# Projecting queries and keys from tokens read in residue order, with joined masks, PSUM-fed pooled sums and a GpSimd scale, in an eight-core decoder layer

## The chip, the cores and the metric

The kernel runs on all 8 cores of one Trainium2 chip. Each core computes 2,048 of the 16,384 tokens of the layer, and reads the 2,048 tokens before them as a halo. The metric is the device time of the slowest core, in microseconds (us).

Some executions fall into a slower state, in which the cores of one die, or of both, have a lower granted TensorE clock. Experiments ran on four chips, called A to D below, and each of them timed the kernel before beside the changed ones. A ratio is the mean time of one kernel's fast runs over the mean of the other's fast runs of the same rounds, so it is not quite the ratio of the medians that are quoted. Intervals are 95% intervals.

## The reference, cut to what matters

```python
ATTN_GROUPS = ((128, 1), (512, 4), (2048, 16))   # (window, dilation) of groups 0, 1, 2; 4 heads of 64 each

def reference(x, ...):                            # x (1, 16384, 1024)
    h = rms_norm(x, g_pre_mix)
    proj = h @ w_in                               # q, k, v (768 columns each), u (256), gates (2 x 1024)
    q, k = apply_rope(q), apply_rope(k)           # t1*cos - t2*sin, t2*cos + t1*sin
    # per group: positions p are split into `dilation` residue streams p mod dilation;
    # within a stream a causal band of 128 steps: softmax(q k / 8) v
    # the three groups are joined by the sums of their softmax denominators
    y_pool = multiscale_pool(u, ...)              # trailing mean over 2/4/8/16 tokens, minus the token
    merged = gate_a * (o_attn @ w_proj_attn) + gate_p * (y_pool @ w_proj_pool)
    x = x + rms_norm(merged @ w_out, g_post_mix)
    h2 = rms_norm(x, g_pre_ffn)
    a, b = split(h2 @ w_gate_up)                  # 2 x 2816
    return x + rms_norm((silu(a) * b) @ w_down, g_post_ffn)
```

Groups 1 and 2 need their queries and keys ordered by residue: all tokens with p mod 4 = 0 first, then 1, 2, 3, and the same modulo 16. The question is which engine should do that shuffle.

## The kernel before

The normed tokens are kept feature-major as `hT` and `hTh` (halo), bf16, 128 partitions x 8 chunks x 2,048 tokens. A first stage norms and transposes the tokens and projects group 2 (12 units of two 8-matmul products, each unit 512 tokens). It ends with the halo part of groups 0 and 1. Four attention stages of 512 tokens follow, `s` = 0 to 3, then the merge, the output projection and the feed-forward part. In the profile PE runs matmuls, DVE is VectorE, ACT ScalarE and POOL GpSimd.

A projection with its rotary step: two products into a pair of PSUM banks, four VectorE products with the cosine and sine tables, and two GpSimd sums. The sums do the shuffle: they read fp32 tiles in steps of 64 bytes (`v_r`) or 16 bytes (`v_rho`) and write contiguous or blocked bf16.

```python
    def rope(ring, wa, wb, rhs, tn, dst_a, dst_b, view, n=512, t0=0):
        tb = tab(tn)
        b = ring.new()
        cos, sin = tb[:, 0, t0:t0 + n], tb[:, 1, t0:t0 + n]
        mm8(b[:, 0, 0:n], wa, rhs)          # 8 matmuls; rhs(k) is the moving operand
        mm8(b[:, 1, 0:n], wb, rhs)
        for dst, fa, fb, op in ((dst_a, cos, sin, ALU.subtract), (dst_b, sin, cos, ALU.add)):
            t = rt.new()
            dve.tensor_tensor(out=t[:, 0, 0:n], in0=b[:, 0, 0:n], in1=fa, op=ALU.mult)
            dve.tensor_tensor(out=t[:, 1, 0:n], in0=b[:, 1, 0:n], in1=fb, op=ALU.mult)
            pool.tensor_tensor(out=dst, in0=view(t[:, 0, 0:n]), in1=view(t[:, 1, 0:n]), op=op)

    v_r = lambda t: t.rearrange("p (a r) -> p r a", r=16)
    v_rho = lambda t: t.rearrange("p (j rho) -> p rho j", rho=4)

    def qk2_unit(kind, s, halo):            # group 2
        # ... (weights and destinations)
        rope(any2, ..., lambda k: src[:, k, s * 512:(s + 1) * 512], s + 4 * halo, da, db, v_r)

    def f1(s, r1, r2):                      # groups 0 and 1, s = -1 (halo) to 3
        # ...
        rhs = lambda k: src[:, k, c0:c0 + 512]
        # ... rope(r2, ..., rhs, tn, ..., v_rho) for q of both groups and k of group 1
```

One attention step, the end of an attention stage, and the pooled branch:

```python
        act.activation(out=pt[:, :, :], in_=sb[:, :, :], func=AF.Exp, scale=0.125)     # att_qk
        for hh in range(2):
            dve.tensor_tensor(out=pt[:, hh, :], in0=pt[:, hh, :], in1=masks[:, mask, :], op=ALU.mult)
        # ...
            dve.tensor_tensor(out=oT2[s % 3][:, pair, :].rearrange(...), in0=val..., in1=den..., op=ALU.mult)
        # ... pooled(s)
                dve.scalar_tensor_tensor(out=zT[p, :], in0=Sx[p, 16:UL], scalar=invw[p, c:c + 1],
                                         in1=X[p, 16:UL], op0=ALU.mult, op1=ALU.subtract)
```

The kernel records all operations first. A list scheduler then orders each engine's instructions from a cost per operation (`op_cost`) and the buffers' lifetimes. All instructions are therefore issued from one or two lines of a helper, and the groups of the profile are told apart by their tiles.

The softmax here doesn't subtract the row's maximum and nothing guards it: scores larger than these inputs give would overflow.

## Time and profile before

The kernel before took 1035.36 us (median of 3, 1034.27 to 1035.75). The profiled execution took 1024.27 us.

| stretch | end | what it holds |
|---|---|---|
| first stage | 146.9 us | norms, transposes, group 2, halo |
| attention, merge, output projection | 547.6 us | stages 0 to 3 and what follows |
| feed-forward | 1022.7 us | matmuls back to back |

The first and second parts of the page: busy time of each engine, then its busy tenths in 40 equal slices of 25.6 us.

```profile
span 1022.7 us, 15344 instructions; the slowest of 8 cores (1018.5 to 1022.7 us)
PE 930.7 (91%) x5520; PEld 472.5 (46%) x5520; DVE 420.4 (41%) x573; ACT 346.4 (34%) x556; POOL 352.7 (34%) x350
...
PE   2779898989787988999989999999999999999993
...
DVE  5668448679998343433455211211112121121111
...
PEclk9899999999999989999999999999999999999997
```

PE is busy at 90% or more in almost every slice of the second half. In slices 11 to 13 it falls to seven or eight tenths, and there, in slices 10 to 12, DVE shows three nines in a row.

Windows of the trace give the same by stretch. The columns are: window and length; busy us (and instructions) of PE, PEld (weight loads), DVE, ACT, POOL; mean granted clock; DMA share; GB/s.

```profile
0.00:150.00 150.00, 114.16 (x849) 76.67 (x850) 88.46 (x144) 85.34 (x161) 66.99 (x55) 0.95 0.71 188
...
225.00:325.00 100.00, 85.89 (x713) 49.21 (x711) 92.55 (x126) 40.46 (x61) 58.39 (x42) 0.97 0.17 30
```

In 225:325, inside attention, VectorE is busy 92.6 of 100 us, and PE 85.9. The groups of instructions show what that consists of (busy us, mean ns of one, then idle time before and what ended it). A matmul's length here is modelled and longer than its spacing: 379 ns stands for a matmul that starts 216 ns after the one before.

```profile
L596 PE MATMUL ps<-hT_68,wq_66_108 128*128 128x512 bf16 x112 | 27.9, 390 | 0.9 <-DVE rt_73_115 L594 0.9
...
L596 PE MATMUL ps<-hT_68,wk_50_92 128*128 128x512 bf16 x56 | 13.4, 379 | 0.0
...
L594 POOL TENSOR_TENSOR q_0_64_106<-rt_73_115 128x512 bf16<-128x512 f32 x5 | 10.8, 2168 | 13.8 <-DVE rt_73_115 L594 12.4 <-DVE uX_88_130 L594 1.4
```

The first line is queries of groups 0 and 1, the second keys of group 2, the third a rope sum of 2.17 us. The view of one tile gives the spread of the mask products (ns, shortest, median, longest):

```profile
L594 DVE TENSOR_TENSOR PT_75_117<-PT_75_117,masks_44 x48: 406/420/3747, 154.4 to 376.6; 128x512 bf16<-128x512 bf16 x48
```

A mask takes 420 ns if nothing disturbs it, yet up to 3,747. The timeline (start us, length us) shows one such meeting:

```profile
242.66 2.15 POOL L594 TENSOR_TENSOR q_0_64_106<-rt_72_114 128x512 bf16<-128x512 f32 x1 [7.24 <-DVE rt_72_114 L594]
243.03 2.40 DVE L594 TENSOR_TENSOR PT_75_117<-PT_75_117,masks_44 128x512 bf16<-128x512 bf16 x2
```

Two masks, 0.84 us by the median, took 2.40 us: the GpSimd sum ran until 244.81, and the masks ended 0.62 us later. The Trainium skill, "SBUF — State Buffer", section Who interferes with whom, describes this as a port pair that VectorE's second SBUF input shares with GpSimd under an exclusive lock, and this trace agrees: on every one of the eight cores 24 of the 96 masks took more than half as long again as the median, and each of them ended 0.28 to 0.29 us after a GpSimd instruction ended.

Weight loads for the values of group 2 read the tokens in steps of 32 bytes, and the tile view has them at 143 ns, where a contiguous load of the same 128x128 takes 98:

```profile
L596 PEld LDWEIGHTS ps<-wv_51_93,hTh_69 x112: 142/143/151, 124.1 to 138.0; 128*128 128x128 bf16 x112
```

The chain of waits that ended last, by engine, as shares of the span:

```profile
PE 72%; DVE 9%; issue 7%; POOL 6%; ACT 5%; DMA 1%; DVEq 0%; POOLq 0%; ACTq 0%; SPq 0%
```

### The profile page before, as it was taken

What the parts mean: (1) busy time and instruction counts of PE and PEld (TensorE: products, weight loads), DVE (VectorE), ACT (ScalarE), POOL (GpSimd) and SP (SyncE); (2) the same over time, 40 slices, a digit from 0 to 9 for tenths busy, and PEclk for the clock granted to TensorE, in tenths of its full rate; (3) what the DMA queues carried; (4) which work ended last, traced back from release to release, by engine and by line L of the source; (5) the groups of instructions that cost most, each with busy time, mean ns of one, the idle gap of its engine ahead of it and who ended that gap; (6) DMA issues with size and microseconds to landing.
All of it is one profiled execution on the core that took longest, in us unless ns stands there. A gap on an engine that the chain in (4) does not pass through costs nothing.

```text
span 1022.7 us, 15344 instructions; the slowest of 8 cores (1018.5 to 1022.7 us)
## 1 busy us (share of the span) xinstructions
PE 930.7 (91%) x5520; PEld 472.5 (46%) x5520; DVE 420.4 (41%) x573; ACT 346.4 (34%) x556; POOL 352.7 (34%) x350
## 2 busy tenths in 40 slices
PE   2779898989787988999989999999999999999993
PEld 2346585556453443444444444444444444444441
DVE  5668448679998343433455211211112121121111
ACT  4686437645343242422766111111101111111110
POOL 1528445344757512333886110111332000001232
PEclk9899999999999989999999999999999999999997
DMA  8868711220061635331777667663323444430321
GB/s 234 261 188 217 172 30 43 31 54 1 1 114 22 99 59 121 62 62 22 208 263 225 117 116 124 119 109 62 124 104 122 83 79 69 80 62 1 124 83 41
DMA packets 30778, 105.02 MB, mean 103 GB/s; under 512 B 3952, under 2 KB 3952, under 8 KB 30704
## 3 DMA queue, kind: packets, MB, share of 16 engines
q0 software_dynamic: 14432, 45.65, 26.9%
q1 hardware_dynamic: 15984, 58.33, 17.1%
q8 instruction: 45, 0.74, 0.3%
q14 instruction: 29, 0.24, 0.1%
q10 hardware_dynamic: 288, 0.06, 0.1%
HBM read 132.90 MB, written 16.78 MB: 146 GB/s over the span
## 4 chain that ended last, share of the span: by engine, by line
PE 72%; DVE 9%; issue 7%; POOL 6%; ACT 5%; DMA 1%; DVEq 0%; POOLq 0%; ACTq 0%; SPq 0%
PE ps L596 63%; PE ps L594 9%; DVE PT_75_117 L594 2%; ACT xsb_53_95 L594 1%; DVE PT_74_116 L594 1%; DVE rt_72_114 L594 1%; DVE zT_134 L594 1%; DVE rt_73_115 L594 1%; DMA xst_37_79<-xo 1%; POOL x1b_101_143 L594 1%; POOL x1b_102_144 L594 1%; DVE hTh_69 L594 1%; POOL x1b_103_145 L594 1%; ACT junk_55_97 L594 1%; ACT PT_75_117 L594 0%
## 5 line engine op out<-in xcount | busy, mean ns | idle before, releaser
L596 PE MATMUL ps<-wdna_155,ffT_154 128*128 128x512 bf16 x512 | 115.7, 379 | 0.0
L596 PE MATMUL ps<-hT_68,wgu_109_151 128*128 128x512 bf16 x420 | 100.4, 379 | 0.0
L596 PE MATMUL ps<-hT_68,wgu_110_152 128*128 128x512 bf16 x420 | 100.4, 379 | 0.0
L596 PE MATMUL ps<-hT_68,wgu_111_153 128*128 128x512 bf16 x392 | 93.7, 379 | 0.0
L596 PEld LDWEIGHTS ps<-wdna_155,ffT_154 128*128 128x128 bf16 x512 | 50.1, 98 | 60.4
L596 PEld LDWEIGHTS ps<-hT_68,wgu_109_151 128*128 128x128 bf16 x420 | 41.0, 98 | 49.3
L596 PEld LDWEIGHTS ps<-hT_68,wgu_110_152 128*128 128x128 bf16 x420 | 41.0, 98 | 49.1
L596 PEld LDWEIGHTS ps<-hT_68,wgu_111_153 128*128 128x128 bf16 x392 | 38.4, 98 | 46.2
L596 PE MATMUL ps<-hT_68,wgs_76_118 128*128 128x512 bf16 x224 | 56.3, 393 | 2.9 <-ACT tg_80_122 L594 1.8
L596 PE MATMUL ps<-hT_68,wgs_77_119 128*128 128x512 bf16 x224 | 53.5, 379 | 2.1 <-ACT tg_81_123 L594 1.0
L594 DVE TENSOR_TENSOR ffT_154<-ps,sa_115_157 128x512 bf16<-128x512 f32 x30 | 20.7, 691 | 79.2 <-PE ps L594 79.2
L594 DVE TENSOR_TENSOR ffT_154<-ps,sa_116_158 128x512 bf16<-128x512 f32 x29 | 20.1, 692 | 78.4 <-PE ps L594 78.4
L594 DVE TENSOR_TENSOR ffT_154<-ps,sa_117_159 128x512 bf16<-128x512 f32 x29 | 20.1, 691 | 77.1 <-PE ps L594 77.1
L594 ACT ACTIVATE sa_115_157<-ps 128x512 f32<-128x512 f32 x30 | 17.9, 598 | 80.1 <-PE ps L594 80.1
L594 ACT ACTIVATE sa_116_158<-ps 128x512 f32<-128x512 f32 x29 | 17.3, 597 | 80.8 <-PE ps L594 80.8
L594 ACT ACTIVATE sa_117_159<-ps 128x512 f32<-128x512 f32 x29 | 17.3, 597 | 78.0 <-PE ps L594 78.0
L594 DVE TENSOR_TENSOR PT_75_117<-PT_75_117,masks_44 128x512 bf16<-128x512 bf16 x48 | 39.6, 864 | 8.6 <-ACT PT_75_117 L594 8.5
L594 ACT ACTIVATE junkd_107_149<-ps 128x1024 bf16<-128x1024 f32 x18 | 18.3, 1016 | 73.2 <-PE ps L594 73.1
L594 DVE SCALAR_TENSOR_TENSOR tg_80_122<-tg_80_122,ps 128x512 f32<-128x512 f32 x32 | 22.0, 689 | 46.8 <-ACT tg_80_122 L594 44.1
L596 PE MATMUL ps<-wdnb_156,ffT_154 128*128 128x512 bf16 x160 | 39.8, 379 | 0.0
L594 DVE SCALAR_TENSOR_TENSOR tg_81_123<-tg_81_123,ps 128x512 f32<-128x512 f32 x32 | 22.0, 687 | 40.4 <-ACT tg_81_123 L594 40.3
L594 ACT ACTIVATE junkd_108_150<-ps 128x1024 bf16<-128x1024 f32 x14 | 14.2, 1017 | 69.4 <-PE ps L594 69.4
(499 smaller groups left out, 1821.6 us busy)
## 6 DMA issues: line engine op xcount, KB each, us to landing
wgu_109_151<-wgu POOLq DMA_DIRECT2D x15, 512.0 KB, 5.8
wgu_110_152<-wgu POOLq DMA_DIRECT2D x15, 512.0 KB, 5.8
wgu_111_153<-wgu POOLq DMA_DIRECT2D x14, 512.0 KB, 5.7
wgs_76_118<-wg POOLq DMA_DIRECT2D x8, 512.0 KB, 5.3
wgs_77_119<-wg POOLq DMA_DIRECT2D x8, 512.0 KB, 6.1
wdna_155<-wdn POOLq DMA_DIRECT2D x8, 512.0 KB, 8.6
tab_70_112<-tab SPq DMA_DIRECT2D x6, 512.0 KB, 6.0
tab_71_113<-tab SPq DMA_DIRECT2D x6, 512.0 KB, 6.1
```

Source lines behind the costliest of these rows:

```text
L594: e.ops.append(lambda q, m=method, a=a, k=k, s=sem.sem, v=step: getattr(q, m)(*a, **k).then_inc(s, v))
L596: e.ops.append(lambda q, m=method, a=a, k=k: getattr(q, m)(*a, **k))
```

## The change

The intent was to take the shuffle off GpSimd, whose sums lock VectorE out, and give it to PE's reads. Each matmul then reads its 512 tokens in residue order, so that PSUM, tables and sums are all contiguous. VectorE is relieved three more ways. The scheduler learns of the shared port.

```diff
 # residue order: PE reads in steps of 16 elements (32 bytes) or 4 elements (8 bytes)
+    by16 = lambda t: t.rearrange("p (a r) -> p r a", r=16)
+    by4 = lambda t: t.rearrange("p (j rho) -> p rho j", rho=4)
-        rope(any2, ..., lambda k: src[:, k, s * 512:(s + 1) * 512], s + 4 * halo, da, db, v_r)
+        rope(any2, ..., lambda k: by16(src[:, k, s * 512:(s + 1) * 512]), tb[:, 0, :], tb[:, 1, :], da, db)
-        rhs = lambda k: src[:, k, c0:c0 + 512]
+        rhs = lambda k: by4(src[:, k, c0:c0 + 512])
+        if s < 0:
+            rhs = lambda k: by16(src[:, k, c0:c0 + 512])
-            pool.tensor_tensor(out=dst, in0=view(t[:, 0, 0:n]), in1=view(t[:, 1, 0:n]), op=op)
+            pool.tensor_tensor(out=dst, in0=fap(t[:, 0, 0:n], w), in1=fap(t[:, 1, 0:n], w), op=op)
 # ... (tables permuted on the host to match; k0 is written through by4 instead)

 # masks in one op, the mask broadcast over the two heads with a zero step
-        for hh in range(2):
-            dve.tensor_tensor(out=pt[:, hh, :], in0=pt[:, hh, :], in1=masks[:, mask, :], op=ALU.mult)
+        dve.tensor_tensor(out=pt[:, :, :], in0=pt[:, :, :], in1=fap(masks[:, mask, :], [(0, 2), (1, 512)]), op=ALU.mult)

 # final scale on GpSimd; pooled sums with the token's term read from PSUM (u), not SBUF (X)
-            dve.tensor_tensor(out=oT2[s % 3][:, pair, :]..., op=ALU.mult)
+            pool.tensor_tensor(out=oT2[s % 3][:, pair, :]..., op=ALU.mult)
-                dve.scalar_tensor_tensor(out=zT[p, :], ..., in1=X[p, 16:UL], ...)
+                dve.scalar_tensor_tensor(out=zT[p, :], ..., in1=u[p, :], ...)

 # scheduler: a VectorE op with two SBUF inputs and a GpSimd op exclude each other
+        if n.port:
+            t = max(t, self.pool.free)
+        elif n.eng is self.pool and not n.dma:
+            t = max(t, self.port_free)
-    return 0.17 + (0.0034 if strided else 0.0021) * n
+    return 0.17 + (0.0040 if strided else 0.0021) * n

 # weight loads of the next stage paced one token tile later
-        if i >= NT and todo and i + 3 < 2 * NT:
+        if i >= NT and todo and i + 4 < 2 * NT:
-            pool.dma(d, w, dsem("d_w01_%d" % len(todo)), after=[sp_x[i + 3]])
+            pool.dma(d, w, dsem("d_w01_%d" % len(todo)), after=[sp_x[i + 4]])
 # ... (smaller moves: two copies to GpSimd, the order of four adds, own semaphores for the last weight loads)
```

## The prediction

> **What bounds the kernel now.** From about 550 us to the end, matmuls run back to back at 216 ns per 128x512 (timeline); nothing in the change reaches that part. Before it PE loses time: from the matmuls' columns at 216 ns per 512 I estimate 118 us of PE idle in the first 500 us, 50 in 0:150 (norms, group-2 queries and keys; DMA share 0.71) and about 50 in 150:325 (attention). There VectorE is tightest: 148.5 of 175 us busy, 92.5 of 100 in 225:325 (busy time by window). Much of that is waiting: a mask multiply takes 0.42 us at the median but up to 3.7; the 96 take 74 us, not 40 (groups by tile). The long ones end when a GpSimd rope sum ends. The Trainium skill ("SBUF — State Buffer", Who interferes with whom) says a VectorE instruction with two SBUF inputs contends with a GpSimd instruction that reads SBUF; the trace agrees: one pair took 2.40 us beside a 2.15 us sum, while products reading PSUM stay at 0.68.
>
> **What changes.**
> - Masks: 96 ops become 48. One alone should take about 0.69 us (0.42 plus 512 bf16 elements at two per cycle, the skill's "VectorE: DVE Perf Modes"; estimate), against 0.84 for two. With fewer waits I expect 74 us to become about 42.
> - Pooled sums: 16 subtractions (16 us, 0.74 to 2.7 each) read PSUM: about 12 us, no waits. A PSUM bank is held longer.
> - Final scale: 8 ops, 16 us (1.3 to 4.9 each), leave VectorE; GpSimd gets about 8 x 1.5 us.
> - Rope sums on GpSimd read contiguous tiles: 1.95 to 2.15 us become about 1.3 (the unstrided k0 form now): some 48 ops, 35 us less, shorter blocks for VectorE.
> - The scheduler now models the shared port and places masks between sums.
> VectorE in 150:325 falls from 148 to about 100 us; PE's work there, about 125 us, becomes the bound.
> - PE: moving operands are read with 32-byte steps (192 matmuls of group 2, and the halo) or 8-byte steps (256 of groups 0 and 1). No moving operand in the trace is read so. Weight loads are: 98 ns contiguous, about 113 with 8-byte steps, 144 with 32-byte steps. If 32-byte steps double a matmul, 46 us of PE work is added, mostly where PE has 50 us of slack; if 8-byte steps do too, another 55 us come in attention and the change loses. I take no penalty as likeliest.
>
> **On the critical path.** Of some 50 us of VectorE and 25 of net GpSimd relief I expect 28 us of the attention stage and 5 of the first to reach the end: about 1003 us. The possible stride penalty skews the range upwards.
>
> **What would show it.** Right: 128x512 matmuls on residue-order tokens still start 216 ns apart; joined masks near 0.7 us, few over 1.5; rope sums near 1.3 us; VectorE busy in attention below 110 us; merge starting some 30 us earlier; the last 450 us unchanged. Wrong: those matmuls 400 ns or more apart; masks still waiting; PE in attention waiting on ACT's exponentials or PSUM banks.
>
> **What would make it wrong.** A stride penalty on moving reads; the broadcast mask losing the two-per-cycle rate (1.2 us each); the scale's long GpSimd op delaying the merge; the new order losing elsewhere; or the attention chain (scores, exponential, mask, values, one score buffer) being latency-bound, so that a freer VectorE buys little.
>
> Chances: faster by over 2% 0.62, within 2% 0.2, slower by over 2% 0.18. Predicted 1003 us, range 975 to 1050.

## The result, and the profile after

The changed kernel is correct and took 1206.06 us (median of its four runs, 1204.56 to 1206.45 in the fast three; one slow run took 1344.45). The kernel before of the same rounds took 1035.29. The ratio is 1.1643 [1.1620, 1.1666]: slower by 16.4%.

```profile
span 1204.9 us, 15240 instructions; the slowest of 8 cores (1199.1 to 1204.9 us)
PE 1138.1 (94%) x5520; PEld 492.8 (41%) x5520; DVE 371.9 (31%) x509; ACT 346.3 (29%) x556; POOL 326.8 (27%) x366
...
PE   3899999899999989899999989999999999999994
...
DVE  5231233041334565553433454122111112221110
...
PEclk9999965677999999899999999999999999999997
```

PE has as many matmuls as before, 5,520, but is busy 207 us longer; DVE, ACT and POOL are busy as long or less. DVE no longer reaches nine tenths in any slice. The sixth to tenth slices show something new: a granted clock of five to seven tenths (the nines before them record nothing, as shown below). The first stage now ends at 303.2 us instead of 146.9, and the output projection at 729.8 instead of 547.6. The feed-forward part takes 475 us in both kernels (729.8 to 1204.9, and 547.6 to 1022.7). The chain of waits is now almost all PE:

```profile
PE 88%; issue 3%; POOL 3%; DVE 2%; ACT 1%; DMA 1%; SPq 0%; POOLq 0%; DVEq 0%; ACTq 0%
```

The same groups as before, and the masks by tile:

```profile
L610 PE MATMUL ps<-hT_68,wq_66_108 128*128 128x512 bf16 x112 | 53.2, 628 | 1.0 <-DVE rt_72_114 L608 1.0
...
L610 PE MATMUL ps<-hT_68,wk_50_92 128*128 128x512 bf16 x56 | 52.8, 1097 | 0.0
...
L608 POOL TENSOR_TENSOR q_0_64_106<-rt_73_115 128x512 bf16<-128x512 f32 x5 | 6.4, 1275 | 33.0 <-DVE rt_73_115 L608 33.0
```

```profile
L608 DVE TENSOR_TENSOR PT_75_117<-PT_75_117,masks_44 x24: 679/694/1758, 314.0 to 594.2; 128x1024 bf16<-128x1024 bf16 x24
```

The rope sum fell from 2.17 to 1.28 us, and the joined mask takes 0.694 us, as intended. But the matmuls that read in steps grew: 56 of them with 32-byte steps went from 13.4 to 52.8 us. The timeline gives their spacing. A line `x7` is seven matmuls and the line after it is the eighth of the same product, so the difference of the two starts, over 7, is the time from start to start.

```profile
111.97 0.93 PE L610 MATMUL ps<-ident_43,xsb_52_94 128*128 128x128 bf16 x7
112.69 0.31 PE L608 MATMUL ps<-ident_43,xsb_52_94 128*128 128x128 bf16 x1
112.79 6.61 PE L610 MATMUL ps<-hT_68,wk_50_92 128*128 128x512 bf16 x7
119.22 1.10 PE L608 MATMUL ps<-hT_68,wk_50_92 128*128 128x512 bf16 x1
...
415.90 3.32 PE L610 MATMUL ps<-hT_68,wq_66_108 128*128 128x512 bf16 x7
419.04 0.63 PE L608 MATMUL ps<-hT_68,wq_66_108 128*128 128x512 bf16 x1
...
420.60 1.68 PE L610 MATMUL ps<-hT_68,wu_111 128*128 128x512 bf16 x7
422.12 0.38 PE L608 MATMUL ps<-hT_68,wu_111 128*128 128x512 bf16 x1
```

With 32-byte steps a matmul starts (119.22 - 112.79) / 7 = 918 ns after the one before. With 8-byte steps it is (419.04 - 415.90) / 7 = 449 ns (451 in the middle of all of them). The contiguous projection at 420.60 still has 217 ns. No wait stands between these matmuls.

The first two lines hold the other new thing. These are transposes of contiguous data, and they start (112.69 - 111.97) / 7 = 103 ns apart, where the kernel before has them 55 ns apart, as its timeline shows:

```profile
87.95 0.55 PE L596 MATMUL ps<-ident_43,xsb_53_95 128*128 128x128 bf16 x7
88.34 0.22 PE L594 MATMUL ps<-ident_43,xsb_53_95 128*128 128x128 bf16 x1
```

This is what half the clock looks like. The windows of the kernel after, for the stretch of the 32-byte steps:

```profile
0.00:150.00 150.00, 123.01 (x290) 32.02 (x291) 45.75 (x73) 49.25 (x85) 15.67 (x20) 1.00 0.43 121
150.00:300.00 150.00, 142.85 (x466) 53.97 (x464) 43.00 (x69) 33.05 (x67) 31.37 (x34) 0.67 0.25 63
```

The clock of the first window reads 1.00 although the transposes there are 103 ns apart: the first clock record of this trace is at 147.6 us, so that figure records nothing. In the second window records exist, with a stretch of 44 us at 0.5, and the mean is 0.67, with PE busy 142.85 of 150 us. The Trainium skill, "TensorE: Matmul & The Clock Gate", section Part 1: The HAM clock gate, puts the half clock down to an idle PE. Here it came with a PE that the profile calls 95% busy.

Is the half clock what makes the stepped matmuls slow? The same trace says no. In a short stretch at full clock (209.0 to 215.9 us by its clock records) the transposes start 59 ns apart by these rounded times, and four matmuls with 32-byte steps last 3.85 us. Less the last one's modelled 1.10 us that is three spacings of 917 ns, the same as at half clock:

```profile
209.68 0.57 PE L610 MATMUL ps<-ident_43,xsb_53_95 128*128 128x128 bf16 x7
210.09 0.22 PE L608 MATMUL ps<-ident_43,xsb_53_95 128*128 128x128 bf16 x1
...
213.74 3.85 PE L610 MATMUL ps<-hTh_69,wk_50_92 128*128 128x512 bf16 x4
```

Over all cores the middle spacing is 918 ns in recorded half clock and 917 in full clock with 32-byte steps, and 453 and 451 with 8-byte steps.

### The profile page after: what moved, and what is told of

Same layout as the page of the kernel before. It is cut to its first block, busy times and chain, and to the rows that moved or that the text cites. A ratio compares the mean times of both kernels' runs of the same rounds, so it can differ in the third digit from the quotient of the medians.

```text
span 1204.9 us, 15240 instructions; the slowest of 8 cores (1199.1 to 1204.9 us)
## 1 busy us (share of the span) xinstructions
PE 1138.1 (94%) x5520; PEld 492.8 (41%) x5520; DVE 371.9 (31%) x509; ACT 346.3 (29%) x556; POOL 326.8 (27%) x366
## 4 chain that ended last, share of the span: by engine, by line
PE 88%; issue 3%; POOL 3%; DVE 2%; ACT 1%; DMA 1%; SPq 0%; POOLq 0%; DVEq 0%; ACTq 0%
PE ps L610 77%; PE ps L608 11%; DMA xst_41_83<-xo 1%; POOL x1b_103_145 L608 0%; POOL x1b_102_144 L608 0%; DVE rt_72_114 L608 0%; POOL x1b_101_143 L608 0%; POOL x1b_104_146 L608 0%; DVE val_67 L608 0%; DVE x1b_102_144 L608 0%; DVE hTh_69 L608 0%; SPq L608 0%; ACT xsb_53_95 L608 0%; ACT PT_75_117 L608 0%; DVE den_135 L608 0%
## 5 line engine op out<-in xcount | busy, mean ns | idle before, releaser
L610 PE MATMUL ps<-wdna_155,ffT_154 128*128 128x512 bf16 x512 | 115.7, 379 | 0.0
L610 PE MATMUL ps<-hT_68,wgu_109_151 128*128 128x512 bf16 x420 | 100.4, 379 | 0.0
L610 PE MATMUL ps<-hT_68,wgu_110_152 128*128 128x512 bf16 x420 | 100.4, 379 | 0.0
L610 PE MATMUL ps<-hT_68,wgu_111_153 128*128 128x512 bf16 x392 | 93.7, 379 | 0.0
L610 PE MATMUL ps<-hT_68,wk_67_109 128*128 128x512 bf16 x112 | 53.2, 629 | 2.1 <-DVE rt_72_114 L608 2.1
L610 PE MATMUL ps<-hT_68,wq_66_108 128*128 128x512 bf16 x112 | 53.2, 628 | 1.0 <-DVE rt_72_114 L608 1.0
L610 PE MATMUL ps<-hT_68,wgs_76_118 128*128 128x512 bf16 x224 | 53.6, 379 | 0.3 <-ACT tg_80_122 L608 0.3
L610 PE MATMUL ps<-hT_68,wgs_77_119 128*128 128x512 bf16 x224 | 53.6, 379 | 0.0
L610 PE MATMUL ps<-hT_68,wq_49_91 128*128 128x512 bf16 x56 | 52.9, 1098 | 0.0
L610 PE MATMUL ps<-hT_68,wk_50_92 128*128 128x512 bf16 x56 | 52.8, 1097 | 0.0
L610 PE MATMUL ps<-hTh_69,wk_50_92 128*128 128x512 bf16 x56 | 52.8, 1097 | 0.0
L608 DVE TENSOR_TENSOR rt_72_114<-ps,tab_71_113 128x512 f32<-128x512 f32 (+1 forms) x32 | 20.9, 662 | 68.5 <-PE ps L608 68.0
L608 ACT ACTIVATE junkd_107_149<-ps 128x1024 bf16<-128x1024 f32 x19 | 19.3, 1016 | 77.8 <-PE ps L608 77.7
L608 ACT ACTIVATE sa_115_157<-ps 128x512 f32<-128x512 f32 x30 | 17.9, 597 | 80.2 <-PE ps L608 80.2
L608 ACT ACTIVATE sa_116_158<-ps 128x512 f32<-128x512 f32 x29 | 17.3, 596 | 81.1 <-PE ps L608 81.1
```

What stands on the lines that cost most here:

```text
L608: e.ops.append(lambda q, m=method, a=a, k=k, s=sem.sem, v=step: getattr(q, m)(*a, **k).then_inc(s, v))
L610: e.ops.append(lambda q, m=method, a=a, k=k: getattr(q, m)(*a, **k))
```

## The experiments

Two theories were on the table after the result.

- Theory A: the moving operand pays by address, so that the byte step of its read slows the matmul. In what unit it pays was open. A1 was a cost for each 4-byte word, at most two of them to a 16-byte line; A2 was that extra dimensions of the pattern cost, whatever the bytes. The count of 16-byte lines used below was fitted after the ladder had run.
- Theory B: the loss lies elsewhere, in the new instruction order (the scheduler's port model, the pacing of the weight loads) or in the half clock, and the slow matmuls only fill time that PE had idle anyway.

| run | chip | what it is | us | before there | ratio |
|---|---|---|---|---|---|
| e1_contiguous_reads | A | after, PE reads contiguous | 996.34 | 1025.19 | 0.9717 |
| e2_undo_order | A | after without residue order | 1007.12 | 1025.19 | 0.9821 |
| e4_32byte_only | A | after, 8-byte reads contiguous | 1146.59 | 1025.19 | |
| e5_step_ladder | A | e1, each unit another step | 1037.91 | 1025.19 | |
| e6_pairs | B | e2 with pairs | 1006.03 | 1025.03 | 0.9816 |
| e8_masks_alone | B | before, joined masks | 1006.94 | 1025.03 | 0.9826 |
| e9_masks_scale_pooled | B | before, masks, scale, pooled | 999.33 | 1025.03 | 0.9752 |
| e10_pairs_at_32_bytes | B | e1, group 2 in pairs | 1036.65 | 1025.03 | |
| e7_order_alone | C | before, residue order only | 1201.38 | 1035.33 | |
| e11_best_pairs | C | e9 with pairs | 1013.06 | 1035.33 | 0.9789 |
| e13_dma_pacing | C | e9 with pacing | 1009.34 | 1035.33 | 0.9748 |
| e14_pacing_and_pairs | D | e9 with pacing and pairs | 991.58 | 1025.50 | 0.9676 |

### The reads made contiguous

This kernel is the changed one, with its instruction mix, tables, scheduler and layout, but PE reads its tokens contiguously. It computes wrong values (relative error 0.095): the queries and keys come out in token order where residue order is expected.

```diff
-    rope(any2, ..., lambda k: by16(src[:, k, s * 512:(s + 1) * 512]), ...)
+    rope(any2, ..., lambda k: src[:, k, s * 512:(s + 1) * 512], ...)
-    rhs = lambda k: by4(src[:, k, c0:c0 + 512])          # and the two by16 reads of the halo
+    rhs = lambda k: src[:, k, c0:c0 + 512]
```

> The changed kernel with one edit: every moving operand is read contiguously (results wrong on purpose: queries and keys get other tokens' columns). Order of instructions on every engine, masks, scale, pooled sums, scheduler stay as changed. Theory A (the byte step of the moving operand slows the matmul, nothing else is wrong): the 128x512 matmuls of queries and keys go back to 216 ns apart, granted clock in the first 450 us back to about 0.95, time about 1000 us (990 to 1012), below the kernel before. Rival B (the new order, the shared-port scheduler, the scale on GpSimd or held PSUM banks cost the time): stays above 1150 us.

It took 996.34 us against 1025.19, ratio 0.9717 [0.9701, 0.9732]. Everything the changed kernel lost comes back, with a gain of 2.8% besides. The matmul spacing is 216 ns again, the clock of all cores is 0.978 to 0.982, and the first stage ends at 144.5 us. One group and one window of it:

```profile
L610 PE MATMUL ps<-hT,wk 128*128 128x512 bf16 x158 | 38.5, 380 | 3.3 <-DVE rt L608 2.3 <-issue 0.6 <-DVE PT L608 0.2
```

```profile
225.00:325.00 100.00, 90.83 (x720) 51.66 (x730) 70.18 (x98) 44.96 (x64) 57.58 (x58) 0.97 0.36 59
```

A key projection again has a modelled length of 380 ns. VectorE in 225:325 is busy 70 us instead of 93. So order, pacing and layout fall as the main cause: they are all still in this kernel. The half clock does not fall by this run, since the clock came back up together with the reads; it falls by the equal spacings at both clocks above.

This is also the case that the prediction took as likeliest, no stride penalty. It expected 1003 us; the run has 996.

### One step size at a time

The kernel after with only the 32-byte reads left (wrong, relative error 0.079):

```diff
-        rhs = lambda k: by4(src[:, k, c0:c0 + 512])
+        rhs = lambda k: src[:, k, c0:c0 + 512]
```

> The changed kernel with the 8-byte-step reads of stages 0 to 3 made contiguous (wrong results on purpose), the 32-byte-step reads of group 2 and of the halo stage kept. Theory A: 256 matmuls fall from 451 to 216 ns apart, 60 us of PE work less, nearly all on the chain: 1145 to 1160 us. If instead the low granted clock of the first stages were the cause, the time would hardly move, as that stage is untouched.

It took 1146.59 us in a single look. Against the contiguous kernel of the same chip the 32-byte steps cost 1146.59 - 996.34 = 150.3 us. From the spacings one can work out 192 + 16 matmuls of 512 columns x 0.701 us (918 less 217 ns), plus 16 of 128 columns x 0.17, which is 149 us. The remaining 8-byte steps cost 1206.06 - 1146.59 = 59.5 us, and 256 x 0.235 us (451 less 216 ns) gives 60 (the kernel after was timed earlier, so this difference is the rougher one). So the kernel grew by the whole excess of its slow matmuls. Two things cancel in this sum: idle time of PE that absorbed part of the excess, and the half clock, which slowed the contiguous matmuls between the slow ones. The traces allow an estimate, matmul by matmul over the first stage of the slowest core: what contiguous matmuls took beyond their spacing at full clock comes to 10 us in the contiguous kernel and 19 here (9 to 11 and 14 to 19 over all cores), and what PE waited besides to 32 and 24 us. So the half clock cost some 9 us, and less waiting gave about as much back.

### The change without the residue order, and the residue order without the rest

> The kernel before plus all parts of the change except the residue-order reads (tokens read in natural order, GpSimd sums read strided as before); results right. Theory A: no slow matmul is left, time 1005 to 1020 us: a gain of 15 to 30 us from masks, pooled sums, scale and scheduler. Rival B: well above 1035 us.

```diff
 # e2: the changed kernel with rope(), qk2_unit(), f1() and the tables of the kernel before
-    rope(any2, ..., lambda k: by16(src[:, k, s * 512:(s + 1) * 512]), tb[:, 0, :], tb[:, 1, :], da, db)
+    rope(any2, ..., lambda k: src[:, k, s * 512:(s + 1) * 512], s + 4 * halo, da, db, v_r)
```

> The kernel before with the residue-order reads alone (tables, k1 layout, contiguous GpSimd sums), nothing else of the change. Theory A: strided matmuls add 192 x 0.701 us (group 2), about 14 us (halo stage) and 256 x 0.235 us = 60: 209 us of PE work; GpSimd's relief gives back some 10: about 1.19 of before (1.18 to 1.20). If part of the loss came from the order together with the joined masks, held PSUM banks or port model, it would be clearly under 1.16.

```diff
 # e7: the kernel before with only the residue order of the change
-        rhs = lambda k: src[:, k, c0:c0 + 512]
+        rhs = lambda k: by4(src[:, k, c0:c0 + 512])
 # ... (by16 in qk2_unit and the halo, permuted tables, contiguous sums)
```

The change without the order is correct and took 1007.12 us, ratio 0.9821 [0.9803, 0.9838]. The order alone is correct and took 1201.38 us in a single look, against 1035.33 on chip C. The order alone is thus as slow as the whole change. As a ratio it is 1.16, below the 1.18 to 1.20 that was expected and at the edge of what was to speak for a part of the loss in other edits; but the kernel before was disturbed on chip C (see below), and the span of 1199.8 us is 1.17 of its undisturbed cores' 1022.

The first of these runs also answers the question. It differs from the kernel with contiguous reads mainly in who shuffles: GpSimd in this one, nobody in that one. So the shuffle costs about 1007.12 - 996.34 = 11 us on GpSimd, against some 210 (1206.06 - 996.34) on PE.

That leaves a question, because the other parts are worth 18 us or more by themselves: where did they go?

The landmarks answer a part of it. The time from the last halo matmul, which ends the first stage, to the end of the output projection is 400.2 us before and 374.1 in the kernel with contiguous reads. The parts other than the steps saved 26 us there. With the 8-byte steps the same stretch takes 426.1 us with all the other parts (the kernel after) and 429.6 without them (the order alone). Of 26 us, some 4 are left. (The scheduler puts a few matmuls of the first attention stage before that landmark, not the same ones in each kernel; evening that out changes these figures by up to 4 us.) In the first stage the other parts even went the wrong way: with the steps it ends at 303.7 us with them and at 295.1 without (298 to 304 and 294 to 296 over the cores), and no run tells which of them costs that. For the attention stages the traces suggest a reason, which is argued: once PE is the slowest engine in that stretch, a freer VectorE only waits. In the groups of the kernel after the masks have 19.0 us of idle time before them, ended by ScalarE's exponentials, against 8.5 before.

### A ladder of steps

To find the law rather than one figure, each of the twelve group-2 units reads with another step and run length (wrong, relative error 0.095). A run of `e` elements is contiguous, and runs lie `step` apart.

```diff
+    LADDER = {("q", 0, 0): (1, 1), ("q", 1, 0): (2, 1), ("q", 2, 0): (4, 1), ("q", 3, 0): (8, 1),
+              ("k", 0, 0): (16, 1), ("k", 1, 0): (32, 1), ("k", 2, 0): (16, 2), ("k", 3, 0): (16, 4),
+              ("k", 0, 1): (16, 8), ("k", 1, 1): (4, 2), ("k", 2, 1): (8, 4), ("k", 3, 1): (8, 2)}
+    step = lambda t: t.rearrange("p (a r e) -> p r a e", r=st_ // run, e=run)
-    rope(any2, ..., lambda k: src[:, k, s * 512:(s + 1) * 512], ...)
+    rope(any2, ..., lambda k: step(src[:, k, s * 512:(s + 1) * 512]), ...)
```

> The contiguous-read kernel (first run of this batch) with one read pattern for each of the twelve group-2 units (wrong results on purpose): single elements at steps of 2, 4, 8, 16, 32 and 64 bytes; runs of 2, 4 and 8 elements at 32-byte steps; runs of 2 at 8 and 16 bytes; runs of 4 at 16 bytes. Theory A1 (one 4-byte word each 0.88 ns, two such slots for a line of 16 bytes that is touched once): 216 ns contiguous, 451 at 4, 8 bytes, about 451 to 917 at 16, 917 at 32 and 64; runs of 2 at 8 bytes 216; runs of 2 at 16 or 32 bytes 451; runs of 4 and 8 at 216. Theory A2 (every extra dimension of the pattern costs, whatever the bytes): all but the plain unit slow alike.

These are the first seven matmuls of some of the units in the timeline. Their length is six spacings and one modelled matmul, so it grows with the spacing:

```profile
27.21 1.67 PE L610 MATMUL ps<-hT,wq 128*128 128x512 bf16 x7
...
59.19 6.16 PE L610 MATMUL ps<-hT,wk 128*128 128x512 bf16 x7
...
74.55 3.34 PE L610 MATMUL ps<-hT,wq 128*128 128x512 bf16 x7
...
82.69 3.38 PE L610 MATMUL ps<-hT,wk 128*128 128x512 bf16 x7
...
90.94 6.46 PE L610 MATMUL ps<-hT,wq 128*128 128x512 bf16 x7
...
117.84 1.77 PE L610 MATMUL ps<-hT,wk 128*128 128x512 bf16 x7
...
121.51 1.67 PE L610 MATMUL ps<-hTh,wk 128*128 128x512 bf16 x7
...
125.94 1.74 PE L610 MATMUL ps<-hTh,wk 128*128 128x512 bf16 x7
```

In order of time: contiguous, 64-byte steps, 8-byte steps, runs of two at 32 bytes, 16-byte steps, runs of four at 32 bytes, runs of eight at 32 bytes, and runs of two at 8 bytes. From the starts of the first and the eighth matmul of a unit (the eighth is not shown):

| pattern of the 512 bf16 columns | 16-byte lines entered | start to start, ns |
|---|---|---|
| contiguous; runs of 8 at 32 bytes | 64 | 216; 216 |
| 4-byte steps; runs of 2 at 8; runs of 4 at 16; runs of 4 at 32 | 128 | 226; 226; 226; 229 |
| 8-byte steps; runs of 2 at 16; runs of 2 at 32 | 256 | 452; 452; 460 |
| 16-byte steps; 32-byte steps; 64-byte steps | 512 | 900; 918; 857 |

The number of lines orders every point. A fit by eye is the larger of 216 ns and 1.76 ns per line entered (256 lines give 451, 128 give 225). It was fitted to this run, and the later kernels that used it (pairs at 8 and at 32 bytes) repeat patterns of the ladder, so it has not been tried on a new one. Theory A1 falls: it gave 451 ns for 4-byte steps, and 226 were measured. Theory A2 falls: runs of eight at 32 bytes have as many dimensions as runs of two, and cost nothing. The 4-byte unit is the weakest point: its first half ran at 427 ns under a halved clock, and only its second half gave 226. The 64-byte figure, 857, lies 5% under the 16-byte one, and why is open.

This is the figure to hold against two sentences of the Trainium skill. "SBUF — State Buffer", in the cachelines box of the section Door 1: The DMA port swizzle, says "how far you can stride for free depends on dtype: 4 fp32, 8 bf16". "Advanced Engine Details and Errata", section Memory Cachelines, says that two hits on a line absorb the access latency. For a moving operand neither holds. An 8-byte step puts two elements in each line and costs 452 ns instead of 216; a step of 8 bf16 elements costs 900. Four elements to a line were needed.

### Is there slack in the first stage?

The prediction had some 50 us of slack for PE there. This kernel is the one with contiguous reads, and lets group 2 read runs of two at 32-byte steps, 460 ns each (wrong, relative error 0.095). It adds 192 x 0.244 = 47 us of PE work to that stage, and the clock should stay up.

```diff
-    lambda k: src[:, k, s * 512:(s + 1) * 512]
+    lambda k: src[:, k, s * 512:(s + 1) * 512].rearrange("p (a r e) -> p r a e", r=8, e=2)
```

> The contiguous-read kernel (0.972 of before) with the 192 group-2 matmuls reading runs of 2 elements at 32-byte steps (wrong results on purpose). By the ladder each takes 460 ns, 47 us of PE work more, and PE stays busy enough that the granted clock is not halved for long. If the first stages have PE slack that absorbs added work: under 25 us more than the contiguous kernel (ratio under 0.997). If there is no slack to speak of: 40 to 50 us more (ratio about 1.01 to 1.02). Against it stands the changed kernel, whose 701 ns more per 32-byte matmul (149 us in all) reached the end in full, 150 us.

A single look took 1036.65 us, against 996.34 for the contiguous kernel, though on another chip (their kernels before took 1025.03 and 1025.19). Of 47 added us 40 reached the end.

```profile
0.00:150.00 150.00, 120.54 (x536) 53.06 (x537) 70.26 (x111) 74.11 (x133) 35.08 (x43) 0.92 0.70 177
```

The clock of the first 150 us was 0.92 here (0.93 in the contiguous kernel) and 0.98 in the next 150, so the loss is not the half clock. It is the lack of slack: the first stage (to the last halo matmul) ends at 186.6 us instead of 145.0, and by the count used above PE's waiting in it fell only from 32 to 25 us (28 to 32 and 25 to 29 over all cores). PE idles in the first stage because transposes wait for norms and loads, and the projections wait in PE's queue in program order; work added to them delays the next transposes. That explanation is argued from the order of the queue; that 40 of 47 us reached the end, and that the waiting hardly shrank, is shown.

### The masks alone, and the three VectorE parts alone

```diff
 # e8: the kernel before with
-        for hh in range(2):
-            dve.tensor_tensor(out=pt[:, hh, :], in0=pt[:, hh, :], in1=masks[:, mask, :], op=ALU.mult)
+        dve.tensor_tensor(out=pt[:, :, :], in0=pt[:, :, :], in1=fap(masks[:, mask, :], [(0, 2), (1, 512)]), op=ALU.mult)
 # e9: e8, and the final scale on GpSimd, and the pooled sums from PSUM
```

> The kernel before with the joined mask alone. If the joined mask is most of the gain of the undone-order kernel (1.8%): 0.985 to 0.992 of before, mask time 74 us to about 45. If the gain needs the scheduler's knowledge of the shared port: within 0.5% of before, with masks still waiting up to 3 us.

> The kernel before with joined masks, scale on GpSimd and pooled sums read from PSUM, but the scheduler as before (no shared port). If the edits themselves make the gain: 0.980 to 0.986 of before, the same as the undone-order kernel's 0.982. If the scheduler's port model makes it: 0.99 or more.

The masks alone took 1006.94 us, ratio 0.9826 [0.9809, 0.9842]. All three together took 999.33, ratio 0.9752 [0.9738, 0.9767]; both are correct, and both are a little better than any of the cases that were expected. The joined mask is the largest single gain, 18 of 26 us. In the second kernel VectorE is no longer the tightest engine of the attention window, and PE is busy 4.8 us more of it than in the kernel before:

```profile
225.00:325.00 100.00, 90.68 (x682) 49.29 (x680) 69.32 (x95) 39.04 (x60) 71.84 (x57) 0.98 0.27 47
```

The three parts without any new scheduling (0.9752) beat the same three parts with the port model and the pacing (0.9821). The intervals do not overlap. These two kernels differ in nothing but those two scheduling edits (the model with its higher cost of a strided sum, and the pacing with its own semaphores for the last weight loads), so together they lost some 7 us.

### Pairs instead of single elements, and the pacing

The ladder suggests a cheaper shuffle. PE reads runs of two at 8-byte steps, which costs 226 ns instead of 216, and GpSimd's sum does the rest with 8-byte instead of 16-byte steps.

```diff
+    pairs2 = lambda t: t.rearrange("p (j r e) -> p r j e", r=2, e=2)
+    v_pair = lambda t: t.rearrange("p (r j e) -> p r e j", r=2, e=2)
-        rope(r2, ..., rhs, tn, rho4(qd[:, g, 0, :]), rho4(qd[:, g, 1, :]), v_rho)      # stages 0 to 3
+        rq = lambda k: pairs2(src[:, k, c0:c0 + 512])
+        rope(r2, ..., rq, tn, rho4(qd[:, g, 0, :]), rho4(qd[:, g, 1, :]), v_pair)
 # ... (k0 written through pairs2; tables of stages 0 to 3 permuted on the host)
```

On top of the change without residue order:

> A correct version built on the undone-order kernel (ratio 0.982 to before): in stages 0 to 3 PE reads pairs of neighbouring tokens at 8-byte steps (order of columns: token mod 4 halved, token div 4, odd or even), tables to match, and GpSimd sorts odd from even with 8-byte steps of fp32. Theory from the ladder (a matmul takes the longer of 216 ns and about 1.76 ns for each 16-byte line that it enters; here 128 lines): the 256 matmuls start 226 ns apart, 3 us more PE work in all. If GpSimd's sums then take about 1.3 instead of 2.1 us, the time falls to 0.973 to 0.980 of before; if GpSimd is as slow at 8-byte steps as at 16 (2.1 us), it stays at 0.982 to 0.985.

It took 1006.03 us, ratio 0.9816 [0.9802, 0.9831]: no different from 0.9821. The undisturbed sums of stages 0 to 3 did fall to 1.50 us, so the gain that was expected for this case did not come; the idle time of VectorE that ended with those sums of queries was 3.1 us without pairs and 3.2 with them. On top of the three VectorE parts, on chip C, together with the three parts plus the pacing edit:

> Correct; a candidate for the best: masks, scale and pooled sums with the scheduler of before (0.9752), plus the pairs of the sixth experiment in stages 0 to 3. If the pairs help by what GpSimd saves (2.1 to 1.5 us for 24 of its sums): 0.970 to 0.974 of before. If GpSimd is off the chain there: 0.975 to 0.977.

> Masks, scale and pooled sums (0.9752) plus the small edit of the change that lets each weight load of groups 0 and 1 wait for one token load more. If this edit is what makes the undone-order kernel (0.982) slower than 0.9752: 0.980 to 0.984, with 5 us more PE idle in 100:150. If the scheduler's port model is: 0.974 to 0.977.

```diff
 # e13: e9, and
-        if i >= NT and todo and i + 3 < 2 * NT:        # ... after=[sp_x[i + 3]]
+        if i >= NT and todo and i + 4 < 2 * NT:        # ... after=[sp_x[i + 4]]
 # ... (own semaphores for the last weight loads)
```

They took 1013.06 us, 0.9789 [0.9765, 0.9813], and 1009.34 us, 0.9748 [0.9727, 0.9770]. Chip C needs care. In runs classed as fast, some cores had a lower clock and were longer, on both dies. The cores view of the pacing kernel has cores 0 and 1 at 1006.4 and 1004.8 us with clocks 0.959 and 0.960, and the six others at 985.1 to 991.0 with 0.986 to 0.988; core 0 has one record of 162 us at a clock of 0.8125. The kernel before has its cores there near 1022 or near 1032 us. The slowest core of chip C is therefore a disturbed one. Undisturbed cores of the pacing kernel (985 to 991 us) are not slower than those of the three parts alone on chip B (993.5 to 997.4), so the pacing is not what lost 7 us. By elimination it is the scheduler's model, or the two edits together; no run tried the model alone. This whole step rests on cores picked by their clock, from different chips, and is weaker than the ratios.

Whether the first measurement's 1035 us for the kernel before, beside 1024.27 for its profiled run, was also a chip with disturbed cores cannot be told: the timed runs left no record of their cores. It would explain why the time lost against the contiguous kernel, about 209 us, agrees with the spacings, while 1206.06 - 1035.29 + 29 us (what the contiguous kernel gains) gives only 200.

### A version that beats both

> Correct; last candidate: masks, scale, pooled sums and the later weight loads (on undisturbed cores of the last batch 985 to 991 us, against 1020 to 1024 for the kernel before), plus pairs in stages 0 to 3. If GpSimd's shorter sums still help there: undisturbed cores at 980 to 986 us, ratio of runs 0.960 to 0.970 on a chip whose cores are all undisturbed. If the new instruction order that the scheduler makes of it loses again, as the pairs did in the last batch (994 to 996 on undisturbed cores): 990 us or more.

The edit is both of the last two on top of the three VectorE parts. It is correct, and took 991.58 us (989.55 to 992.97) against 1025.50, ratio 0.9676 [0.9659, 0.9694]. This is faster than the kernel before by 3.2%, and better than every other kernel here.

```profile
225.00:325.00 100.00, 97.66 (x755) 54.23 (x754) 65.25 (x93) 42.62 (x65) 65.86 (x64) 1.00 0.37 64
```

```profile
L594 DVE TENSOR_TENSOR PT<-PT,masks x48: 681/693/2027, 144.0 to 374.9; 128x1024 bf16<-128x1024 bf16 x48
```

PE is busy 97.7 of 100 us in the window that had 85.9 before, and VectorE 65 instead of 93 (the same stretch of time, not quite the same work). How the last 8 us (from 999.33) split between pacing and pairs is not settled: the undisturbed cores point to the pacing for most of it, and no fair pair of runs isolates the pairs there.

## Why the prediction was right or wrong

The prediction was 1003 us with a range of 975 to 1050. The result was 1206 us: the prediction was wrong, and mainly by one step.

- **The step that failed: "I take no penalty as likeliest."** The moving operand does pay for steps. The runs show 451 ns with 8-byte and 918 ns with 32-byte steps, instead of 216, and taking only the steps away gives 996 us. The prediction had named this penalty as the first thing that would make it wrong, and its sign, matmuls 400 ns or more apart, is what was seen.
- **The size of the penalty if there was one.** "If 32-byte steps double a matmul, 46 us" was too small: they more than quadruple it, and cost 150 us (1146.59 - 996.34). Only for the 8-byte steps was doubling right: 55 us was the estimate, and 59.5 were measured.
- **"Mostly where PE has 50 us of slack."** There was next to none: 40 of 47 added us of PE work reached the end, at full clock. Time in which PE waited for its inputs was not room for more work on it here.
- **The hint was in the prediction.** It cites weight loads at 98, about 113 and 144 ns. An engine whose reads are known to slow down with the step should not get "no penalty" as its likeliest case for its other operand. The hint gave the sign but not the size: a 32-byte step adds 46% to a weight load and 325% to a matmul's spacing (918 over 216).
- **Right: the masks.** Expected were 0.69 us each and about 42 us in all; the kernel after has 0.694 at the median and 42.2 in all. The rate of two bf16 elements per cycle ("VectorE: DVE Perf Modes", section Mode 2×_1P), on which that estimate rests, holds with the mask broadcast by a zero step over the outer dimension: the second 512 elements add 0.274 us.
- **Right: pooled sums and rope sums.** 12 us were expected for the pooled sums and 11.9 measured; about 1.3 us for a contiguous rope sum and 1.27 measured. The final scale on GpSimd takes 1.34 to 1.36 us in seven cases of eight (1.80 in the other) where 1.5 was expected.
- **Right under its own assumption: the sum.** Without a stride penalty 33 us were expected, and 29 are found on chip A (1025.19 - 996.34). That it fits so closely is partly luck: the three VectorE parts gave 26, the contiguous sums about 11, and the scheduling edits, which the prediction did not count as a loss, took some 7 back.
- **Right: the last part.** 475 us from the first feed-forward matmul to the end in both kernels.
- **Missed: the scheduler's part.** "The new order losing elsewhere" was named as a risk and is, by the elimination above, real but small, some 7 us.
- **Missed: the half clock.** In the kernel after the clock was halved through much of the first stage. It did not slow the stepped matmuls (918 and 917 ns), and cost the contiguous ones some 9 us by the estimate above, which less waiting gave back. No run halves the clock by itself. That slow, line-bound matmuls look like little activity to whatever grants the clock is argued only.

The probabilities were part of the mistake. "Slower" got 0.18, although the text itself says that if both step sizes cost, "the change loses".

## What to carry to other kernels

A layout shuffle is not free because it moves into an access pattern: for a matmul's moving operand count the 16-byte lines that it enters, and keep at least four bf16 elements in each (226 ns for 512 columns here; two in each cost 452, one 900). When a change puts work on the engine that holds 72% of the chain of waits to relieve one that holds 9%, measure that work first by a ladder of sizes inside one kernel. And gains of a relieved engine exist only where that engine binds: 26 us saved in the attention and merge stages shrank to some 4 once PE had become slower.

## What the Trainium skill lacked or had wrong

- "SBUF — State Buffer", section Door 1: The DMA port swizzle (box on cachelines), and "Advanced Engine Details and Errata", section Memory Cachelines: two hits per 16-byte line are not enough for a matmul's moving operand. Two hits cost 452 ns for 512 columns, one hit 900, and only four hits came near the contiguous 216 (226). "8 bf16" as a free stride is wrong for it by a factor of 4.2 (900 over 216).
- "TensorE: Matmul & The Clock Gate" gives no cost for the moving operand's step. The runs show the larger of 216 ns and about 1.76 ns per line entered (a fit to one run), independent of the number of dimensions, and the same at half clock where the lines bind. Nor does it give the weight load's: 98 ns contiguous, 143 at 32-byte steps.
- The same page, Part 1, ties the half clock to an idle PE. Here the granted clock averaged 0.67 over 150 us in which PE was busy 142.85 (as the profile models it), with 32-byte steps.
- "GPSIMD Engine Reference", section 7 (Performance pitfalls for Q7 kernels), has a cost for inner steps above 8 bytes alone, in kernels written for those cores. The built-in rope sum here took 1.27 us contiguous and 1.50 with 8-byte fp32 steps, and 1.95 to 2.15 with 16 or 64 bytes: 8 bytes are cheaper, but not free.
- No page says that the clock records of a trace can begin late, and that a mean before them then records nothing: the first record of the kernel after is at 147.6 us, and it showed 1.00 over its first 150 us, while its transposes started 103 ns apart instead of 55.
